# Modulation tiles on GpSimd, ScalarE and VectorE in place of TensorE in a two-layer trunk, and a first feed-forward with wide gate and up

## Chip, core and metric

The kernel runs on one core of a Trainium2 chip. Its time is the device time of one execution in microseconds (us), as the median of three runs. The engines are TensorE (PE in the profile; PEld is its weight load), VectorE (DVE), ScalarE (ACT) and GpSimd (POOL); SyncE's queue (SP) issues the DMAs of the weights. TensorE writes to banks of PSUM; everything else lies in SBUF.

## The reference

One sequence of 256 positions with 1024 channels in fp32 goes through two layers. Layer 0 is a mixer (a state-space half and an attention half with one output projection) and a gated feed-forward; layer 1 is a convolution module and another such feed-forward. Ahead of every sub-layer the norm is modulated by a vector c, and its output is gated by it:

```
mod = silu(c) @ mod_w + mod_b          # per layer: 6 sections of 1024 (shift, scale, gate, twice)
h = rms_norm(x, g) * (1 + scale) + shift
x = x + gate * sub_layer(h)

# conv feed-forward, 2816 hidden channels
a = causal_dwconv(h @ w_gate, conv_w, conv_b)     # width 3
y = (silu(a) * (h @ w_up)) @ w_down
```

So mod_w takes 1024 x 6144 weights of each layer for one row of results: a weight is read once and used once. Every 128 outputs of a section are one tile here.

## The kernel before

**Weights.** All weights come as chunks of 128x1024 fp32 (512 KB), in the sequence of `chunk_order` (line 89), into `raw` buffers (10, and later four more cut from the tiles `ABT`). `pump` (line 604) issues the next load on SyncE's queue as soon as a buffer is given back by `done`. For fp32 accuracy a chunk is split: ScalarE copies it to a rounded upper part (`whi`, or `whim` in six-slot stages), VectorE subtracts that from the chunk (`wlo`, `wlom`), and the buffer is free. TensorE then multiplies the upper part by both parts of the activations and the lower part by the upper one.

**Narrow and wide.** `tile_mm` (697) does this with three matmuls of 256 columns into 256 columns of a bank. `tile_wide` (704) does the first two as one matmul of 512 columns into a 512-wide bank; its two halves are added when the bank is emptied. Before, ffn1's gate and up are wide, ffn0's narrow.

**Gate and up.** A feed-forward has 22 pairs of a gate and an up column (the first three columns go through `lead`, the other 41 through `run_seq`). Four banks rotate. For a gate, ScalarE copies the bank to `g` and VectorE does two taps of the convolution (`ac`); for an up, VectorE multiplies the bank by `ac` (`uu`), and ScalarE and VectorE split the product into `hv`, which the down projection reads.

**Modulation.** A chunk of mod_w has one of two forms. An "mp" chunk holds rows: `mod_pe` (664) multiplies it on TensorE with silu(c) (`csv`) as the stationary operand, two matmuls of 512 columns a chunk; `mod_evac` copies the result to `mrow`, and `mod_sel` turns it into columns of `modv` by 8 small matmuls. The mixer has 24 mp chunks (three sections). An "md" chunk holds the transpose: `mod_dve` (651) multiplies it on VectorE by `cb` (silu(c) on every partition), with the sum of every row accumulated straight into a column of `modv`. ffn0 has 32 md chunks among its weights, ffn1 8.

**Order.** The class Plan records all operations of a part, gives them costs and ranks, and `arrange` (490) writes one fixed list for every engine, in which an operation's group name may add a number from the table `BONUS` to its rank. On the chip each engine executes its list in order, waiting where an operand isn't there.

Of the kernel before, what the change touches and what calls it, by code (L numbers as in the profile page):

```python
# [12 lines left out]
F32 = mybir.dt.float32  # L13
# [3 lines left out]
OP = mybir.AluOpType  # L17
# [7 lines left out]
RAW_BUFS = 10  # L25
# [10 lines left out]
MD_STEP = (2, 1)  # L36
LN_MODS = [(1, 3), (1, 4)]
# [31 lines left out]
BONUS = {'a-evac': 335.5, 'a-gate_tail': -31, 'a-h_u': 30.1, 'a-lead': 1098.9, 'a-low': -73.8, 'a-mod_dve': -8, 'a-modulate': 1999.9, 'a-norm_r': -982.9, 'a-norm_y': 306, 'a-post': 445.1, 'a-pump': 954.6, 'a-split_hi': -425.7, 'a-up_tail': 66.2, 'ab0': -12.4, 'ab1': 314.2, 'abt0': 146.2, 'abt1': -30.4, 'b': 279, 'b-low': -73, 'b-mod_dve': -176.4, 'b-post': 911.4, 'b-split_hi': -11, 'b-up_tail': 886.8, 'c-conformer': -25.6, 'c-low': -9.1, 'c-mod_dve': -195.6, 'c-norm_gain': 25.4, 'c-pump': 219.6, 'c-residual': 320.9, 'c-shift_cols': 229.2, 'c-split_hi': 308.1, 'c-stat_acc': -1.4, 'c-stat_sq': 101.1, 'c-warm': -558.3, 'ca0': -152.1, 'ca1': -12.7, 'clear0': 157.9, 'clear1': -261, 'clear2': -759.1, 'clear4': 44.9, 'cond': -26.1, 'cond0': -12.1, 'cond1': 42.8, 'cond2': 691.8, 'd-first': -7, 'd-h_u': -580.7, 'd-lead_evac': -586.6, 'd-low': 4.5, 'd-modulate': 635.9, 'd-norm_r': 37.7, 'd-norm_y': -60.3, 'd-post': -2.9, 'd-pump': -138.1, 'd-split_hi': 154.2, 'd-tap': -33.8, 'drive0': 1.6, 'drive1': -4.5, 'e-conformer': 85.9, 'e-conv_get': -2.1, 'e-conv_pe': -40.1, 'e-first': 81.1, 'e-last': -52.8, 'e-low': 930.5, 'e-post': 456.3, 'e-pump': 891.4, 'e-split_hi': -462.7, 'e-tap': -6.2, 'e-warm': 194.3, 'exp0': 1252.5, 'exp2': 21.4, 'exp3': -345.5, 'f-centre': 2, 'f-conformer': 9.6, 'f-conv_pe': 446.2, 'f-stat_sq': 551.5, 'feat0': 57.3, 'feat1': -197.8, 'feat2': -30.4, 'feat3': 36.9, 'feat4': 24.8, 'feat5': 605.8, 'feat6': 5.8, 'feat7': 416.6, 'fin0': 397.6, 'fin1': 2.4, 'fin2': 50.6, 'fin3': 2.6, 'g-conformer': -42.5, 'g-ffn_open': 117.6, 'g-h_u': -3, 'g-low': 5.9, 'g-mod_evac': -461.8, 'g-mod_sel': 153.6, 'g-norm_gain': 93, 'g-norm_y': 146.6, 'g-raw_h': -0.7, 'g-residual': 1.4, 'g-shift_cols': 5.7, 'g-silu': -1090.8, 'g-split_hi': 479.6, 'g-stat_acc': 1.7, 'g-stat_sq': 51.3, 'g-warm': -23.3, 'gelu': 585.4, 'glub0forbin': -413.2, 'gneg': 205.2, 'h-evac': -6.5, 'h-gate_tail': 1.1, 'h-h_u': -76.3, 'h-lead': -618.6, 'h-low': -370.8, 'h-modulate': 34.2, 'h-norm_r': -20.3, 'h-norm_y': -12.8, 'h-post': -171.7, 'h-pump': -339.6, 'h-split_hi': -7.9, 'h-up_tail': 9.5, 'i-gate_tail': -2.7, 'i-mod_dve': -975.6, 'i-post': -1.7, 'i-pump': -16.6, 'i-split_hi': -142.8, 'i-up_tail': -1.1, 'j-ffn': 118.4, 'j-finish': -2.7, 'j-low': -4.4, 'j-norm_y': 10.7, 'j-pump': -302, 'j-residual': -1.8, 'j-split_hi': -44.7, 'j-stat_acc': 2.3, 'j-stat_sq': 12.3, 'j-warm': -6, 'k_evac1': -9.9, 'k_evac2': -1.3, 'k_evac3': -335.2, 'kd': 9.3, 'loada000': 8500, 'loada001': 8400, 'loada010': 8200, 'loada011': 8100, 'loada020': 7900, 'loada021': 7800, 'loada030': 7600, 'loada031': 7500, 'loada040': 7200, 'loada041': 7100, 'loada050': 6900, 'loada051': 6800, 'loada060': 6600, 'loada061': 6500, 'loada070': 6300, 'loada071': 6200, 'loadabo0': -405.2, 'loadabo1': 81.4, 'loadabo2': 3.3, 'loadabo3': -114.5, 'loadabo4': 1631.5, 'loadabo6': 873.6, 'loadabo7': 639.8, 'loadanti': 29.1, 'loadbc': 7300, 'loadc': 9500, 'loadglu0': 978.9, 'loadglu1': -21.6, 'loadid': 9499, 'loadk0': 547.5, 'loadk2': 27.5, 'loadk3': -47.2, 'loadmp02': -5.7, 'loadmp04': -2.6, 'loadmp13': -566.2, 'loadmp14': 62.4, 'loadpp': 8600, 'loadsel': 9498, 'loaduq0': 8300, 'loaduq1': 8000, 'loaduq2': 7700, 'loaduq3': 7400, 'loaduq4': 7000, 'loaduq5': 6700, 'loaduq6': 6400, 'loaduq7': 6100, 'loadv0': 14.3, 'loadv1': -17.3, 'loadv3': -1548.8, 'loadx0': 9000, 'loadx1': 8900, 'loadx2': 8800, 'loadx3': 8700, 'main0': -164.3, 'main2': -8.5, 'main3': 451.8, 'main4': -14, 'main5': 1.2, 'main6': -581.6, 'main7': 334.9, 'mod_evac': 206.6, 'mod_pe004': -918.1, 'mod_pe048': -322.3, 'mod_pe1': -2043.3, 'mod_pe2': 329.2, 'mod_sel': -10.5, 'mods0': -34, 'mods1': 38.1, 'mods2': 124.4, 'mods3': -9.3, 'mods4': 662.6, 'mods5': -1.9, 'mods6': 23.2, 'mods7': 909.6, 'norm': 145.2, 'norm0': 28.9, 'norm2': 757.3, 'norm3': 4.6, 'out0': -31.3, 'out1': 223.1, 'out3': 13.8, 'poles': -82.2, 'powers': 11, 'proj_k0': 328.4, 'proj_k1': 867.2, 'proj_k2': 38.7, 'proj_k3': -5.7, 'proj_o4firstrue': -1097.9, 'proj_o5': 0.3, 'proj_v0': -1856.4, 'proj_v1': 126.3, 'proj_v2': 30.2, 'proj_v3': -27.8, 'q_evac': 594.3, 'rel': 10.1, 'res0': 6.4, 'res1': 73.3, 'res3': 272.4, 'res4': -210.4, 'rot0': -161.2, 'rot1': -1.6, 'rot2': -1.8, 'score0': -405.2, 'score1': 774.7, 'score2': -648.6, 'score3': -9, 'set': 365.8, 'skip': -738.2, 'splitabo4': 198.9, 'splitabo5': -114.3, 'splitabo6': -1.7, 'splitabo7': -2, 'splitglu1': 472.4, 'splitk1': 258.3, 'splitk3': 63.3, 'splitv0': -27.5, 'splitv1': -12.3, 'splitv3': 231.8, 'sq0': 614.4, 'sq1': 573.3, 'sq2': 839.8, 'sq3': -0.7, 'state': -231.2, 'turn0': -5.9, 'turn1': 10, 'turn3': -406.8, 'u201': -353.5, 'u_evac': -80.8, 'y0': -1280.6, 'y1': -876.8, 'y2': -545.4, 'y3': -191.1}  # L69
# [19 lines left out]
def chunk_order():  # L89
# [7 lines left out]
    def mp(l, s):  # L97
        return [("mp", l, s, f) for f in range(8)]

    a, b, c = mp(0, 2), mp(0, 4), mp(0, 3)  # L100
    order += [("k", 0), ("k", 1)] + a[:4] + [("k", 2), ("k", 3)] + a[4:]
    order += [("v", 0), ("v", 1)] + b[:4] + [("v", 2), ("v", 3)] + b[4:] + c
    order += [("abo", 4), ("abo", 5), ("glu", 0), ("glu", 1)]
# [174 lines left out]
class Plan:  # L278
# [74 lines left out]
    def cost(self, op):  # L353
        eng, fn, a, k, _ = op
        if fn == "dma_start":
            b = self.size(a[0]) * a[0].shape[0] * 4
            return max(1.0 if op[4] == "rel" else 0.06, b / 370e3)
# [191 lines left out]
class Emit:  # L549
    def __init__(self, ctx, tc, nc, d, order):  # L550
# [13 lines left out]
        self.raw = {}  # L564
        self.slots = {}
# [84 lines left out]

    def mod_dve(self, c):
# [820 lines left out]
    def ffn(self, l, mids={}):  # L1472
        nc, v = self.nc, self.nc.vector
        hv = self.hv
        def post(c, ps):
# [3 lines left out]
            if t == "gate":  # L1479
                nc.scalar.activation(g[:, 2:], ps[:, 0:T], AF.Copy)  # L1480
                if l == 1:
                    ps = g[:, 2:]
                    v.tensor_tensor(ps, psw[:, T:2 * T], ps, op=OP.add)
                self.gate_tail(l, i, ps)
            else:
                if l == 1:
                    nc.scalar.activation(u, ps[:, T:2 * T], AF.Copy)
                    v.tensor_tensor(u, ps[:, 0:T], u, op=OP.add)
                    ps = u
# [5 lines left out]
        self.run_seq(ffn_seq(l)[3:], self.h, post, mids=mids, wide=("gate", "up") if l == 1 else ())  # L1495
# [274 lines left out]
    def start(self):  # L1770
# [31 lines left out]
        nc.group = ""  # L1802

# [14 lines left out]
    def mixer0(self, ctx):  # L1818
# [3 lines left out]
        with self.tc.tile_pool(name="mix", bufs=1) as mix:  # L1822
# [11 lines left out]
            self.arena = t([128, ARENA], F32, name="arena")  # L1834
            self.cut = 0
# [30 lines left out]
            self.split(("k", 2))  # L1866
            nc.group = "proj_k1"
# [11 lines left out]
            nc.group = "mod_pe004"  # L1879
            self.mod_pe(fg, 0, fb, 0, 4)  # L1880
# [200 lines left out]
```

## Time and profile before

| what | us |
|---|---|
| median of 3 runs (their range) | 650.72 (647.98 to 651.05) |
| profiled execution, its own time | 652.1 |
| span of the profile | 650.3 |
| TensorE busy | 640.4 |
| VectorE busy | 538.8 |
| ScalarE busy | 404.9 |
| GpSimd busy | 41.2 |

The span is that of one execution between its first and its last instruction; 1.8 us lie around it. Busy times are unions over the span. The mixer ends at about 137 us, ffn0's gate and up run from about 160 to 282, its down projection to 344, the convolution module to 464, ffn1's gate and up from 473 to 583. Because a helper records every operation, almost all rows carry one line (L487); groups are told apart by the names of tiles, `out<-in`.

### The profile page before, as it was taken

How to read it: one execution, taken by the hardware profiler on the slowest of the kernel's cores; microseconds unless marked ns; L12 is line 12 of the kernel's file. 1: busy time of each engine (PE TensorE's matmuls, PEld its weight loads, DVE VectorE, ACT ScalarE, POOL GpSimd, SP SyncE). 2: the span in 40 equal slices, each digit the busy share in tenths (PEclk: the TensorE clock that was granted, in tenths of full speed). 3: DMA queues.
4: the chain of work that ended last, by engine and by line, in shares of the span. 5: the costliest groups of instructions: out<-in, count | busy, mean ns of one | idle time of the engine just before them, and what ended most of it. 6: DMA issues, size and time to landing. Idle time of an engine off the chain costs nothing.

```text
span 650.3 us, 13240 instructions
## 1 busy us (share of the span) xinstructions
PE 640.4 (98%) x5128; PEld 562.5 (87%) x5128; DVE 538.8 (83%) x1059; ACT 404.9 (62%) x736; POOL 41.2 (6%) x99
## 2 busy tenths in 40 slices
PE   8999999999999999999999999999999999999995
PEld 5789876899999999998899987568988888888885
DVE  8698996389999999999657999559999998997641
ACT  3479528897966666654446843377687766675431
POOL 4830000000000000000000222000000000000000
PEclk9999999999999999999999999999999999999998
DMA  8996888765489999999662798496476668764001
GB/s 325 405 377 224 291 324 300 316 217 210 134 288 320 325 331 303 338 328 365 195 196 81 245 325 245 154 380 263 135 280 199 201 214 259 217 210 164 1 0 66
DMA packets 45702, 158.50 MB, mean 244 GB/s; under 512 B 5535, under 2 KB 7112, under 8 KB 45640
## 3 DMA queue, kind: packets, MB, share of 16 engines
q1 hardware_dynamic: 43912, 153.84, 67.6%
q0 software_dynamic: 1152, 3.49, 1.9%
q8 instruction: 40, 0.66, 0.4%
q10 hardware_dynamic: 576, 0.33, 0.2%
q14 instruction: 22, 0.18, 0.1%
HBM read 153.10 MB, written 1.06 MB: 237 GB/s over the span
## 4 chain that ended last, share of the span: by engine, by line
PE 88%; DVE 7%; ACT 2%; DMA 1%; issue 1%; DVEq 0%; SPq 0%
PE bank L487 88%; DVE arena L487 4%; DVE wlo L487 1%; DMA raw<-w_in 1%; ACT CA L487 1%; DVE CS L487 1%; DVE U L487 1%; ACT whi L487 0%; ACT ABT L487 0%; DVE gp L487 0%; DVE nm L487 0%; DVE junk L487 0%; DVE h L487 0%; DVEq L2044 0%; DVE nt L487 0%
## 5 line engine op out<-in xcount | busy, mean ns | idle before, releaser
L487 PE MATMUL bank<-h,whi 128*128 128x256 f32 (+2 forms) x960 | 202.3, 303 | 0.2
L487 PEld LDWEIGHTS bank<-h,whi 128*128 128x128 f32 x960 | 152.4, 189 | 8.7 <-issue 1.0
L487 PE MATMUL bank<-h,wlo 128*128 128x256 f32 (+1 forms) x560 | 155.5, 283 | 0.0
L487 PE MATMUL bank<-h,whim 128*128 128x256 f32 (+1 forms) x664 | 149.1, 311 | 0.0
L487 PE MATMUL bank<-h,wlom 128*128 128x256 f32 x416 | 116.4, 281 | 0.0
L487 PEld LDWEIGHTS bank<-h,whim 128*128 128x128 f32 x664 | 108.2, 189 | 7.7
L487 PEld LDWEIGHTS bank<-h,wlo 128*128 128x128 f32 x560 | 104.5, 189 | 1.3 <-DVE CS L487 0.8
L487 DVE TENSOR_TENSOR wlo<-raw,whi 128x1024 fp32r<-128x1024 f32 x69 | 84.1, 1222 | 13.6 <-ACT whi L487 10.4
L487 ACT ACTIVATE whi<-raw 128x1024 fp32r<-128x1024 f32 x69 | 72.5, 1055 | 20.7 <-PE bank L487 13.7
L487 DVE TENSOR_TENSOR wlom<-raw,whim 128x1024 fp32r<-128x1024 f32 x60 | 72.9, 1222 | 10.5 <-ACT whim L487 10.3
L487 PEld LDWEIGHTS bank<-h,wlom 128*128 128x128 f32 x416 | 78.3, 188 | 0.1
L487 ACT ACTIVATE whim<-raw 128x1024 fp32r<-128x1024 f32 x60 | 62.6, 1054 | 22.7 <-PE bank L487 15.8
L487 PE MATMUL bank<-hv,whim 128*128 128x512 f32 (+1 forms) x236 | 67.7, 351 | 0.0
L487 PE MATMUL bank<-hv,whi 128*128 128x512 f32 x160 | 56.3, 393 | 0.0
L487 PE MATMUL bank<-hv,wlom 128*128 128x256 f32 x192 | 53.9, 281 | 0.0
L487 PEld LDWEIGHTS bank<-hv,whim 128*128 128x128 f32 x236 | 41.3, 189 | 6.2
L487 PE MATMUL bank<-hv,wlo 128*128 128x256 f32 x160 | 44.7, 279 | 0.0
L487 DVE SCALAR_TENSOR_TENSOR ac<-g,pp,ac 128x256 f32<-128x256 f32 x88 | 42.2, 482 | 2.5 <-ACT ac L487 0.8
L487 DVE SCALAR_TENSOR_TENSOR x<-bank,modv,x 128x256 f32<-128x256 f32 x54 | 25.6, 481 | 19.7 <-PE bank L487 19.1
L487 ACT ACTIVATE whi<-ABT 128x1024 fp32r<-128x1024 f32 x28 | 29.3, 1054 | 16.3 <-PE bank L487 15.3
L487 ACT ACTIVATE g<-bank 128x256 f32<-128x256 f32 x40 | 15.3, 382 | 36.4 <-PE bank L487 36.3
L487 PEld LDWEIGHTS bank<-hv,wlom 128*128 128x128 f32 x192 | 36.4, 190 | 0.0
(220 smaller groups left out, 1071.6 us busy)
## 6 DMA issues: line engine op xcount, KB each, us to landing
raw<-w_in SPq DMA_DIRECT2D x213, 512.0 KB, 5.3
ABT<-w_in SPq DMA_DIRECT2D x71, 512.0 KB, 4.9
a<-ap POOLq DMA_DIRECT2D x24, 142.0 KB, 5.4
x<-x_in SPq DMA_DIRECT2D x4, 256.0 KB, 4.2
arena<-scr SPq DMA_DIRECT2D x1, 1024.0 KB, 6.0
cb<-c_in SPq DMA_DIRECT2D x2, 512.0 KB, 4.9
kT<-bc_in SPq DMA_DIRECT2D x1, 512.0 KB, 11.4
out<-junk SPq DMA_DIRECT2D x2, 256.0 KB, 2.0
```

The lines of the kernel that those rows point to most:

```text
L487: getattr(getattr(self.nc, eng), fn)(*a, **k)
```

## The change

In the mixer the 24 mp chunks become md chunks, spread among the weights of k, v, the output projection and the gate of the state-space half. `mod_next` places them one by one among the mixer's groups. Of every three, two go through the new `mod_pool`: GpSimd multiplies the chunk by `cbm` in place, then ScalarE copies it onto itself with the sum of every row accumulated into `modv`. The third is a VectorE multiplication with accumulation, as in `mod_dve`. That is 16 tiles on GpSimd and ScalarE, 8 on VectorE; `mod_pe`, `mod_evac` and `mod_sel` go from the mixer. `broadcast` makes `cbm` at the start, with one VectorE instruction, two matmuls and two ScalarE copies, and the room for it is taken from the raw buffers (9 for 10).

In both feed-forwards every second md chunk goes through `mod_pool`: 16 of 32 in ffn0, 4 of 8 in ffn1. ffn0's gate and up use `tile_wide`, with the addition of the halves as in ffn1: one more VectorE instruction for a gate, and one more of VectorE and of ScalarE for an up. The planner's cost of a DMA changes from 370 to 390 KB a us, and most numbers of the table `BONUS` are new.

```diff
-RAW_BUFS = 10
+RAW_BUFS = 9
...
+MIX_MOD = (1, 1, 0)
+ON_POOL = (1, 0)
...
-    a, b, c = mp(0, 2), mp(0, 4), mp(0, 3)
-    order += [("k", 0), ("k", 1)] + a[:4] + [("k", 2), ("k", 3)] + a[4:]
-    order += [("v", 0), ("v", 1)] + b[:4] + [("v", 2), ("v", 3)] + b[4:] + c
-    order += [("abo", 4), ("abo", 5), ("glu", 0), ("glu", 1)]
+    md = [("md", 0, s, f) for s in (2, 4, 3) for f in range(8)]
+    for c, n in zip([("k", 0), ("k", 1), ("k", 2), ("k", 3), ("v", 0), ("v", 1), ("v", 2), ("v", 3),
+                     ("abo", 4), ("abo", 5), ("glu", 0), ("glu", 1)], (1, 1, 1, 1, 2, 2, 2, 2, 3, 3, 3, 3)):
+        order += [c] + md[:n]
+        del md[:n]
...
-            return max(1.0 if op[4] == "rel" else 0.06, b / 370e3)
+            return max(1.0 if op[4] == "rel" else 0.06, b / 390e3)
...
-                (self.mod_dve if c[0] == "md" else self.split)(c)
+                (self.mod if c[0] == "md" else self.split)(c)
...
+    def mod(self, c):
+
+        self.i_mod += 1
+        (self.mod_pool if ON_POOL[self.i_mod % len(ON_POOL)] else self.mod_dve)(c)
+        if c[3] == 7:
+            self.mod_bias(*c[1:3])
+
+    def mod_pool(self, c):
+        _, l, s, f = c
+        w = self.raw[c]
+        self.nc.gpsimd.tensor_tensor(w, w, self.cb, op=OP.mult)
+        self.nc.scalar.activation(w, w, AF.Copy, accum_out=self.modv[l][:, s * 8 + f:s * 8 + f + 1])
+        self.done(c)
+
+    def mod_next(self, n):
+        for _ in range(n):
+            i = self.i_next
+            self.nc.group = "mod%d" % i
+            c = ("md", 0, (2, 4, 3)[i // 8], i % 8)
+            if MIX_MOD[i % len(MIX_MOD)]:
+                self.mod_pool(c)
+            else:
+                w = self.raw[c]
+                self.nc.vector.scalar_tensor_tensor(w, w, 1.0, self.cb, op0=OP.mult, op1=OP.mult,
+                                                    accum_out=self.modv[0][:, c[2] * 8 + c[3]:c[2] * 8 + c[3] + 1])
+                self.done(c)
+            self.i_next += 1
...
-                if l == 1:
-                    ps = g[:, 2:]
-                    v.tensor_tensor(ps, psw[:, T:2 * T], ps, op=OP.add)
+                ps = g[:, 2:]
+                v.tensor_tensor(ps, psw[:, T:2 * T], ps, op=OP.add)
...
-        self.run_seq(ffn_seq(l)[3:], self.h, post, mids=mids, wide=("gate", "up") if l == 1 else ())
+        self.run_seq(ffn_seq(l)[3:], self.h, post, mids=mids, wide=("gate", "up"))
...
+    def broadcast(self):
+
+        nc = self.nc
+        cb = self.cb.rearrange("p (a b) -> p a b", b=128)
+        nc.vector.tensor_tensor(cb, self.ident.unsqueeze(1).to_broadcast([128, 8, 128]),
+                                self.cs.unsqueeze(2).to_broadcast([128, 8, 128]), op=OP.mult)
+        parts = (0, 4, self.aux[2]), (4, 8, self.aux[1])
+        for a, b, ps in parts:
+            nc.tensor.matmul(ps, self.ones, self.cb[:, a * 128:b * 128], start=True, stop=True)
+        for a, b, ps in parts:
+            nc.scalar.activation(self.cb[:, a * 128:b * 128], ps, AF.Copy, scale=float(D))
...
             self.split(("k", 2))
+            self.mod_next(2)
             nc.group = "proj_k1"
...
-            nc.group = "mod_pe004"
-            self.mod_pe(fg, 0, fb, 0, 4)
+            self.mod_next(1)
             nc.group = "proj_k2"
...
             nc.group = "score0"
             self.attn_score(0, B[0:2])
+            self.mod_next(2)
             nc.group = "proj_v3"
```

GpSimd's list in the mixer, from the end of the constants of the state-space half (`D`) to the turn of the bias table (the COPY of `arena`), before and then after the change:

```order
L487 COPY D_127<-arena 128x1024
L487 MEMSET D_127 128x16
L487 COPY arena<-arena 128x8x128
L487 MEMSET g_0_1641 128x2
```

```order
L491 COPY D_126<-arena 128x1024
L491 MEMSET D_126 128x16
L491 TENSOR_TENSOR raw_75<-raw_75,cbm 128x1024
L491 TENSOR_TENSOR raw_77<-raw_77,cbm 128x1024
L491 TENSOR_TENSOR raw_72<-raw_72,cbm 128x1024
L491 TENSOR_TENSOR raw_74<-raw_74,cbm 128x1024
...
L491 TENSOR_TENSOR ABT_87<-ABT_87,cbm 128x1024
L491 COPY arena<-arena 128x8x128
L491 TENSOR_TENSOR ABT_86<-ABT_86,cbm 128x1024
```

Ten multiplications now stand ahead of the COPY, the first two ahead of the copies of u on ScalarE, and six behind it.

ScalarE's list at the same place: `kT` and `KD` are the attention's keys and a table of the state-space half, `whi_78<-raw_69` the split of v's first chunk, the rows with `modv` the accumulations of `mod_pool`. Before and after:

```order
L487 ACTIVATE kT<-bank_65 128x256 x2
L487 ACTIVATE U_122<-u 32x4x64 x9
L487 ACTIVATE KD<-bank_65 32x16x32 x4
L487 ACTIVATE whi_79<-raw_69 128x1024
L487 ACTIVATE whi_83<-raw_71 128x1024
```

```order
L491 ACTIVATE raw_72,modv_89<-raw_72 128x1024
L491 ACTIVATE kT<-bank_65 128x256 x2
L491 ACTIVATE raw_77,modv_89<-raw_77 128x1024
L491 ACTIVATE raw_76,modv_89<-raw_76 128x1024
L491 ACTIVATE KD<-bank_65 32x16x32 x4
L491 ACTIVATE raw_74,modv_89<-raw_74 128x1024
L491 ACTIVATE raw_75,modv_89<-raw_75 128x1024
L491 ACTIVATE ABT_87,modv_89<-ABT_87 128x1024
L491 ACTIVATE whi_78<-raw_69 128x1024
```

Accumulations stand between and ahead of what was consecutive before: ten ahead of the split of v's first chunk, four of them earlier than these rows.

VectorE's list in ffn0's gate and up, about one pair (`ac`: the taps of the gate, `wlom`: splits, `junk,modv`: a modulation tile, `hv`: the product's lower part), before and after:

```order
L487 SCALAR_TENSOR_TENSOR ac_1643<-g_0_1641,pp,ac_1643 128x256 x2
L487 TENSOR_TENSOR wlom_1634<-ABT_87,whim_1633 128x1024
L487 TENSOR_TENSOR uu_1645<-bank_62,ac_1643 128x256
L487 SCALAR_TENSOR_TENSOR junk,modv_90<-raw_75,cb 128x1024
L487 TENSOR_TENSOR hv<-uu_1645,hv 128x256
L487 TENSOR_TENSOR wlom_1636<-raw_78,whim_1635 128x1024
L487 SCALAR_TENSOR_TENSOR junk,modv_90<-raw_69,cb 128x1024
```

```order
L491 TENSOR_TENSOR g_0_1627<-bank_61,g_0_1627 128x256
L491 TENSOR_TENSOR wlom_1620<-raw_71,whim_1619 128x1024
L491 SCALAR_TENSOR_TENSOR ac_1629<-g_0_1627,pp,ac_1629 128x256 x2
L491 TENSOR_TENSOR uu_1631<-bank_62,uu_1631 128x256
L491 SCALAR_TENSOR_TENSOR junk,modv_90<-raw_74,cb 128x1024
L491 TENSOR_TENSOR uu_1631<-uu_1631,ac_1629 128x256
L491 TENSOR_TENSOR wlom_1622<-raw_73,whim_1621 128x1024
L491 TENSOR_TENSOR hv<-uu_1631,hv 128x256
```

Two sums of bank halves (`g<-bank,g` and `uu<-bank,uu`) come into a pair, and about every second modulation tile goes out of it. In all 11 such tiles stand in gate and up after the change; 12 of ffn0's 16 GpSimd multiplications stand ahead of the last `hv`.

## Rows read from the trace of the kernel before

**Rows 1.** The page, parts 1 and 4: busy time by engine, the chain by engine.

```profile
PE 640.4 (98%) x5128; PEld 562.5 (87%) x5128; DVE 538.8 (83%) x1059; ACT 404.9 (62%) x736; POOL 41.2 (6%) x99
...
PE 88%; DVE 7%; ACT 2%; DMA 1%; issue 1%; DVEq 0%; SPq 0%
```

**Rows 2.** The chain in order of time: start, length (us), what.

```profile
44.81 1.06 ACT CA L487
...
90.05 1.15 DVE wlo L487
91.24 328.39 PE bank L487 x2956
```

**Rows 3.** Stretches of the span: length, busy us of each engine, clock, DMA.

```profile
core 0: us, PE busy (x) PEld busy (x) DVE busy (x) ACT busy (x) POOL busy (x), PEclk, DMA share, GB/s
45.00:57.00 12.00, 12.00 (x100) 10.99 (x97) 9.55 (x21) 11.86 (x20) 0.00 (x0) 1.00 0.87 319
...
57.00:100.10 43.10, 43.01 (x358) 33.63 (x360) 41.97 (x83) 22.44 (x48) 1.10 (x1) 1.00 0.73 257
100.00:137.00 37.00, 37.00 (x510) 30.15 (x501) 17.70 (x43) 30.75 (x78) 0.00 (x0) 0.95 0.80 301
160.00:282.00 122.00, 122.00 (x1024) 121.82 (x1023) 120.83 (x204) 82.51 (x144) 0.00 (x0) 1.00 0.85 291
282.00:344.00 62.00, 62.00 (x382) 55.47 (x382) 46.51 (x69) 30.06 (x41) 0.08 (x1) 1.00 0.77 263
473.00:583.00 110.00, 110.00 (x629) 96.12 (x628) 102.77 (x181) 80.11 (x148) 0.00 (x0) 1.00 0.70 225
```

**Rows 4.** Timeline of GpSimd (POOL) and VectorE (DVE): start, length (us).

```profile
28.21 0.22 POOL L487 TENSOR_TENSOR arena<-arena 128x16 f32<-128x16 f32 x1
...
28.56 0.96 POOL L487 TENSOR_SCALAR arena<-arena 128x16 f32<-128x16 f32 x1
...
28.41 1.00 DVE L487 TENSOR_TENSOR arena<-arena 128x768 f32<-128x768 f32 x1
...
37.48 1.11 POOL L487 COPY D<-arena 128x1024 f32<-128x1024 f32 x1
...
37.80 0.81 DVE L487 SCALAR_TENSOR_TENSOR gp<-modv,gneg 128x1 f32<-128x1 f32 x1
...
27.83 0.15 DVE L487 SCALAR_TENSOR_TENSOR gp<-modv,gneg 128x1 f32<-128x1 f32 x1
```

**Rows 5.** ScalarE's groups, 100 to 137 us: count, busy us, mean ns.

```profile
L487 ACT ACTIVATE whi<-raw 128x1024 fp32r<-128x1024 f32 x4 | 4.2, 1056 | 2.5 <-PE bank L487 1.3 <-DMA raw<-w_in 1.2
...
L487 ACT ACTIVATION_READ_ACCUMULATOR CS<-CS,U 128x1 f32 x11 | 2.1, 190 | 0.0
```

**Rows 6.** Instructions with csv (PE, PEld, ACT, POOL), then mrow (PE, PEld, DVE, ACT).

```profile
100.00:137.00 37.00, 4.49 (x42) 0.97 (x32) 0.00 (x0) 0.00 (x0) 0.95 0.80 301
...
100.00:137.00 37.00, 2.07 (x16) 2.02 (x16) 0.00 (x0) 1.05 (x2) 0.95 0.80 301
```

**Rows 7.** Instructions with cb (DVE, ACT), then with a bank (PE, PEld, DVE, ACT).

```profile
160.00:282.00 122.00, 30.66 (x50) 1.04 (x1) 1.00 0.85 291
...
473.00:583.00 110.00, 8.69 (x15) 0.35 (x1) 1.00 0.70 225
...
57.00:100.10 43.10, 43.01 (x358) 33.63 (x360) 7.00 (x12) 7.90 (x19) 1.00 0.73 257
...
473.00:583.00 110.00, 110.00 (x629) 96.12 (x628) 17.05 (x41) 15.25 (x41) 1.00 0.70 225
```

**Rows 8.** Timeline of ScalarE: gates in ffn0 (eleven), then in ffn1 (nine).

```profile
204.49 0.39 ACT L487 ACTIVATE g<-bank 128x256 f32<-128x256 f32 x1 [1.42 <-PE bank L487]
...
261.44 0.39 ACT L487 ACTIVATE g<-bank 128x256 f32<-128x256 f32 x1 [1.40 <-PE bank L487]
...
503.49 0.39 ACT L487 ACTIVATE g<-bank 128x256 f32<-128x256 f32 x1 [0.89 <-PE bank L487]
...
548.42 0.39 ACT L487 ACTIVATE g<-bank 128x256 f32<-128x256 f32 x1
```

More of the change, by code (lines that the diff above doesn't have):

```diff
@@ L98, in mp @@
         return [("mp", l, s, f) for f in range(8)]
-    a, b, c = mp(0, 2), mp(0, 4), mp(0, 3)
-    order += [("k", 0), ("k", 1)] + a[:4] + [("k", 2), ("k", 3)] + a[4:]
-    order += [("v", 0), ("v", 1)] + b[:4] + [("v", 2), ("v", 3)] + b[4:] + c
-    order += [("abo", 4), ("abo", 5), ("glu", 0), ("glu", 1)]
+    md = [("md", 0, s, f) for s in (2, 4, 3) for f in range(8)]
[3 more added lines that the diff above has]
+        del md[:n]
+    assert not md
     order += [("abo", i) for i in (6, 7, 0, 1, 2, 3)]
@@ L564, in __init__ @@
         self.raw = {}
+        self.i_mod = 0
+        self.i_next = 0
         self.slots = {}
@@ L646, in feed, with mod_bias @@
                     break
-                (self.mod_dve if c[0] == "md" else self.split)(c)
+                (self.mod if c[0] == "md" else self.split)(c)
             self.pos += 1
         self.auto = True
+    def mod(self, c):
[22 more added lines that the diff above has]
+            self.i_next += 1
+    def mod_bias(self, l, s):
+        mc = self.modcols(l, s)
+        self.nc.vector.tensor_tensor(mc, mc, self.par("modb", l * 48 + s * 8, 8), op=OP.add)
     def mod_dve(self, c):
@@ L656, in mod_dve @@
         self.done(c)
-        if f == 7:
-            mc = self.modcols(l, s)
-            self.nc.vector.tensor_tensor(mc, mc, self.par("modb", l * 48 + s * 8, 8), op=OP.add)
     def low(self, n):
@@ L1480, in post @@
                 nc.scalar.activation(g[:, 2:], ps[:, 0:T], AF.Copy)
-                if l == 1:
-                    ps = g[:, 2:]
-                    v.tensor_tensor(ps, psw[:, T:2 * T], ps, op=OP.add)
+                ps = g[:, 2:]
+                v.tensor_tensor(ps, psw[:, T:2 * T], ps, op=OP.add)
                 self.gate_tail(l, i, ps)
             else:
[L1486 to L1489, printed above, removed]
+                nc.scalar.activation(u, ps[:, T:2 * T], AF.Copy)
+                v.tensor_tensor(u, ps[:, 0:T], u, op=OP.add)
+                ps = u
                 nc.scalar.activation(a, a, AF.Silu)
@@ L1784, in start @@
             nc.tensor.matmul(self.mm[i % 4][:, 0:n], self.zero[:, 0:128], self.zero[:, 0:n], start=(i < 4), stop=False)
+        nc.group = "bcast"
+        self.broadcast()
         nc.group = "poles"
@@ L1834, in mixer0 @@
             self.arena = t([128, ARENA], F32, name="arena")
+            self.cb = t([128, 1024], F32, name="cbm")
             self.cut = 0
@@ L1889, in mixer0 @@
             self.pump()
+            self.mod_next(1)
             nc.group = "proj_k3"
             self.proj_k(3)
-            nc.group = "mod_pe048"
-            self.mod_pe(fg, 0, fb, 4, 8)
+            self.mod_next(1)
             nc.group = "splitv0"
@@ L1899, in mixer0 @@
             self.k_evac(3)
+            self.mod_next(1)
             nc.group = "splitv1"
@@ L1912, in mixer0 @@
             vb = B[4:6]
+            self.mod_next(1)
             nc.group = "proj_v0"
@@ L1916, in mixer0 @@
             self.split(("v", 2))
+            self.mod_next(1)
             nc.group = "proj_v1"
@@ L1920, in mixer0 @@
             self.split(("v", 3))
-            nc.group = "mod_pe1"
-            self.mod_pe(fg, 1, fb)
+            self.mod_next(2)
             nc.group = "proj_v2"
             self.proj_v(2, vb)
+            self.mod_next(1)
             nc.group = "score0"
             self.attn_score(0, B[0:2])
+            self.mod_next(2)
             nc.group = "proj_v3"
@@ L1931, in mixer0 @@
                 nc.scalar.activation(self.v[:, t_, :], vb[t_], AF.Copy)
-            nc.group = "mod_pe2"
-            self.mod_pe(fg, 2, fb)
+            self.mod_next(1)
             nc.group = "exp0"
             self.attn_exp(0, B[0:2])
+            self.mod_next(1)
             nc.group = "norm0"
@@ L1939, in mixer0 @@
             self.attn_score(1, B[2:4])
-            nc.group = "mod_evac"
-            self.mod_evac(fb)
+            self.mod_next(1)
             nc.group = "exp1"
             self.attn_exp(1, B[2:4])
+            self.mod_next(1)
             nc.group = "y0"
             self.s5_y(0, B[4])
-            nc.group = "mod_sel"
-            self.mod_sel(fg, B[0])
+            self.mod_next(1)
             nc.group = "norm1"
@@ L1951, in mixer0 @@
             self.attn_turn(0, (B[6], B[7]))
+            self.mod_next(1)
             nc.group = "y1"
             self.s5_y(1, B[5])
+            self.mod_next(1)
             nc.group = "out0"
             self.attn_out(0, B[1])
+            self.mod_next(1)
             nc.group = "score2"
             self.attn_score(2, B[2:4])
+            self.mod_next(1)
             nc.group = "exp2"
             self.attn_exp(2, B[2:4])
+            self.mod_next(1)
             nc.group = "turn1"
             self.attn_turn(1, (B[6], B[7]))
+            self.mod_next(1)
             nc.group = "y2"
@@ L1965, in mixer0 @@
             self.attn_norm(2)
+            nc.group = "mod_bias"
+            for i in (2, 4, 3):
+                self.mod_bias(0, i)
             nc.group = "out1"
```

2 lines of the change are left out of this document (1 added, 1 removed).

## The prediction

> **What bounds the kernel now.** I read the page first, then the chain of waits in order of time, then the busy time of each engine by stretches, because averages over the span mix stages with different limits. By the page TensorE is busy for 98% of the span and the chain runs over it for 88% [rows 1], which invites the thought that work taken off TensorE shortens the kernel by its own length. The chain in order of time says something else for the first 91 us: up to there its pieces are ScalarE's (the row at 44.81 us is the first of a run of them) and then VectorE's, and only from 91.24 us on is TensorE alone on it for 328 us [rows 2]. The stretches agree. Between 57 and 100 us VectorE is busy for 41.97 of 43.10 us; from 100 to 137 us it is at 17.70 of 37.00, with ScalarE at 30.75; in the first feed-forward's gate and up (160 to 282 us) TensorE is at 122.00 of 122.00 and VectorE at 120.83, so there two engines are full at once; in the down projection (282 to 344) and in ffn1 (473 to 583) VectorE has room, 15.5 and 7.2 us [rows 3]. So VectorE has 1.1 us to spare in each of the two stretches where the change puts work beside it.
>
> **What a GpSimd instruction costs VectorE.** The trace of before has almost no GpSimd work, but what it has meets VectorE. A TENSOR_TENSOR of 16 elements takes 0.22 us; a TENSOR_SCALAR of the same size that begins 0.15 us after a VectorE instruction with two operands in SBUF takes 0.96, and ends (28.56 + 0.96 = 29.52) 0.11 us after that one (28.41 + 1.00). The other way round, while GpSimd's COPY of 128x1024 runs (37.48 + 1.11 = 38.59), a VectorE instruction on one column takes 0.81 us in place of its 0.15, and ends at 38.61 [rows 4]. I read this as one access that both need and that one instruction holds to its end. Then a multiplication on GpSimd is not free for VectorE: it costs VectorE the time T that it holds the access, less what VectorE can do meanwhile with operands from a bank.
>
> T has no row, so it is bounded. The COPY streams 1024 elements in 1.11 − 0.22 = 0.9 us [rows 4]. If the multiplication streams as the COPY does, T = 0.9; if its two reads and its write follow one another, 2.7; with the two reads in turn and the fixed part, 2 × 0.9 + 0.2 = 2.0. I take 2.0, since the COPY has one read and the multiplication two.
>
> The Trainium skill bears on this in two places, and both speak against the change. "SBUF — State Buffer", section "Who interferes with whom", says that the pair of ports that VectorE and GpSimd share is locked for a whole instruction, and that a VectorE instruction with two SBUF inputs meets a GpSimd one that reads SBUF; the trace agrees for the small instructions above, and no row shows it for a multiplication. "GPSIMD Engine Reference", section "3.1 Elementwise — side-by-side cycle accounting", gives 4497 ns for a tensor_tensor of 2048 elements on GpSimd; half of it, an estimate of 2.25 us, would put the sum below 4 us higher.
>
> By T = 2.0 a tile that goes to GpSimd holds VectorE for some 1.6 us, while the same tile on VectorE takes 1.23 (30.66 us for 25 pairs of multiplication and accumulator read [rows 7]).
>
> **The mixer.** TensorE loses 4.49 us of modulation matmuls after 100 us and 2.07 of the selection [rows 6], 6.6 in all; those ahead of 91 us lie beside VectorE's chain and give nothing. VectorE gains 8 tiles, GpSimd 16, and ScalarE 16 accumulations of 1.06 + 0.19 = 1.25 us (a 128x1024 ACTIVATE and an accumulator read [rows 5]). Where they fall I take from the order of the instructions.
> - 45 to 57 us: two GpSimd multiplications, whose accumulations stand on ScalarE ahead of the copies of u. ScalarE is at 11.86 of 12.00 [rows 3] and on the chain [rows 2], so these two cost 2 × 1.25 = **+2.5**. VectorE has 2.5 us idle there, which hides the 3.2 us of their hold but for less than a microsecond, beside ScalarE's delay.
> - 57 to 100 us: eight more stand ahead of GpSimd's COPY of the bias table, and VectorE takes one tile. A hold doesn't stop VectorE's instructions with a bank operand, 7.00 of its 41.97 us [rows 7], nor its few reductions, so I charge 0.8 of T: 8 × 2.0 × 0.8 = 12.8, plus 1.2, less the 1.1 idle: **+12.9**. ScalarE is at 22.44 of 43.10 and takes its eight accumulations in that room.
> - 100 to 137 us: TensorE gives 6.6 back if nothing else is late. VectorE has room for its seven tiles (17.70 + 8.6). ScalarE gets four accumulations and loses 1.05 of evacuation: 30.75 + 5.0 − 1.05 = 34.7 of 37, so no more than **−2.3** can be had.
>
> Together +13.1. The broadcast at the start is a VectorE multiplication of 128x1024, two matmuls and two ScalarE copies; at most 1.2 [rows 7] + 2 × 0.5 [rows 6] = 2.2 us with its matmuls beside that, if all of it were on the chain; a gain is excluded, since it only adds work. The chain there is TensorE's, so I take 0. One raw buffer less costs 0 as long as the queue stays ahead; its cover is the buffers loaded ahead, and without it the chunks come late (the fourth case below).
>
> **ffn0.** A pair of gate and up takes (261.44 − 204.49)/10 = 5.695 us narrow, and in the wide form of ffn1 (548.42 − 503.49)/8 = 5.616 [rows 8]. For 20.5 pairs TensorE needs 115.1 in place of 116.7 us, **−1.6**. VectorE in the wide form: ffn1's 102.77 less 8.69 of modulation [rows 3, 7] is 94.1 over 110/5.616 = 19.6 pairs, 4.80 a pair, so 98.4 for 20.5; this holds the added sums of the halves, since ffn1 has them. By the order 11 tiles stay on VectorE inside gate and up, 11 × 1.23 = 13.5, and 12 stand on GpSimd ahead of the last product: 12 × 2.0 × 0.83 = 19.9 (0.83 is what is left beside the bank operands, 17.05 of 102.77 [rows 3, 7]). Sum 131.8, over TensorE's 115.1 by 16.7. Four banks rotate, so TensorE can be three ahead, 1.5 pairs or 8.4 us, and that much of the lag is taken up in the down projection, where VectorE has 15.5 us of room. 16.7 − 8.4 = 8.3 remain; with −1.6 the stage is **+6.7**. The down projection itself (4 tiles on each engine, +3 us on VectorE against 15.5 of room) and ffn1 (4 of 8 tiles moved, +1.7 against 7.2) cost 0.
>
> **Sum.** The profiled execution took 652.1 us; 652.1 + 13.1 + 6.7 = 671.9. The median of the runs is 1.4 lower, so 670.5, rounded to **670**.
>
> **The rivals.**
> 1. *No hold.* The multiplication doesn't block VectorE, or VectorE slips its work between. Then VectorE's 98.4 + 13.5 = 111.9 stays below TensorE's 115.1 and the mixer keeps TensorE's saving: −2.3 − 1.6, that is 648.2, or 647 by the median; with all 6.6 back, 642.5. For it speaks that most GpSimd instructions of before are too small to tell. Against it speaks the column instruction above, which waited out the whole COPY. It decides below T of about 0.6 us, where 8 × 0.8 × T makes up the 3.9 gained. This is the one on the other side.
> 2. *Hold as short as the COPY's*, T = 0.9: mixer 5.8 + 0.1 + 2.5 − 2.3 = +6.1; in ffn0 111.9 + 9.0 = 120.9 is 5.8 over TensorE, which the banks absorb, −1.6. 656.6, or 655 by the median. For it: the only 1024-element rows of GpSimd; against: those have one input.
> 3. *Everything in turn*, T = 2.7, nothing absorbed by the banks and nothing saved by TensorE, because ScalarE executes in order: its accumulations wait for GpSimd, with the copies for v's splits behind them, and a raw buffer comes back only after both engines, so the queue of weights runs late. Mixer 17.3 + 0.1 + 2.5 = +19.9; ffn0 138.8 − 115.1 − 1.6 = +22.1: 694.1, or 693 by the median. For it: ten accumulations stand on ScalarE ahead of the copy for v's first split. Against: ScalarE is at half in that stretch [rows 3].
>
> **How the numbers follow.** I give the forecast 0.54, the first rival 0.23, the second 0.13, the third 0.10. A difference of 0.5% (3.3 us) is about what a measurement of this kernel can tell from none. The forecast and the third are slower; of the second 0.08 is slower and 0.05 the same; of the first 0.20 is faster and 0.03 the same. So slower 0.72, same 0.08, faster 0.20. The range goes from 643, which takes in most of the first rival, to 690, which leaves out the upper end of the third.
>
> **What would show it.** Right: GpSimd multiplications of about 2 us, VectorE's two-operand instructions behind them that end with them and are stretched by as much, VectorE's pieces on the chain past 91 us and again in the gate and up, and a pair period there of 6 us or more. The mixer's last VectorE piece would come some 13 us later. Wrong: VectorE's 1024-element subtractions still at 1.22 us beside running multiplications (no hold), or a pair period of 5.6 us; ScalarE with long waits for GpSimd and the loads late would be the third rival. My forecast fails most easily on T and on the share of the holds that falls where VectorE has no room.

## The result and the profile after

The changed kernel takes 699.12 us (median of four runs, 695.61 to 703.06) against 650.84 for the kernel before: a ratio of 1.0754, with a 95% interval from 1.0683 to 1.0826. It is slower by 48 us, where 20 were forecast, and lies outside the range of 643 to 690.

The page of the profiled execution (its span is 699.3 us) shows TensorE no longer full and its share of the chain down from 88% [rows 1] to 55%. By itself that share doesn't show a loss: in the first experiment below it is 63%, at 651 us. VectorE gains 68 us of busy time.

```profile
PE 645.8 (92%) x4692; PEld 555.2 (79%) x4692; DVE 607.0 (87%) x1077; ACT 445.1 (64%) x829; POOL 152.1 (22%) x135
...
PE 55%; DVE 19%; ACT 5%; issue 3%; DMA 1%; DVEq 0%; SPq 0%; ACTq 0%
```

The stretches that answer to [rows 3], and ffn0's gate and up where they now lie (206 to 332), columns as there:

```profile
45.00:57.00 12.00, 6.29 (x46) 5.06 (x44) 11.41 (x22) 11.06 (x18) 10.16 (x9) 0.85 0.46 176
57.00:100.10 43.10, 36.15 (x307) 33.94 (x307) 41.78 (x55) 26.57 (x52) 17.63 (x7) 0.88 0.71 246
100.00:137.00 37.00, 22.44 (x193) 17.69 (x196) 36.90 (x54) 19.07 (x50) 15.92 (x6) 0.72 0.47 167
206.00:332.00 126.00, 117.99 (x636) 100.49 (x634) 123.72 (x182) 85.27 (x160) 32.22 (x11) 0.96 0.74 256
```

VectorE is as full from 57 to 100 us as it was, but gets through 55 instructions in place of 83. The full stretch doesn't end there: from 100 to 137 us, where it was half idle, it is now busy for 36.90 of 37.00, and TensorE waits. In gate and up it is full too, and TensorE is not.

The timelines of GpSimd and VectorE at the first three multiplications show why (start, length in us; the row with x3 is three in a row):

```profile
48.28 7.01 POOL L491 TENSOR_TENSOR raw<-raw,cbm 128x1024 f32<-128x1024 f32 x3
...
48.54 2.17 DVE L491 TENSOR_TENSOR arena<-CS,arena 128x16 f32<-128x16 f32 x1
50.74 2.28 DVE L491 TENSOR_TENSOR CS<-arena 128x16 f32<-128x16 f32 x1
53.06 2.36 DVE L491 TENSOR_TENSOR arena<-CS,arena 128x16 f32<-128x16 f32 x2
55.45 0.19 DVE L491 TENSOR_TENSOR CS<-arena 128x16 f32<-128x16 f32 x1
```

VectorE has products of 16 elements to do, 0.19 us each when nothing is in the way (55.45). Each of them waits out a whole multiplication, gets through in the gap, and the next meets the next multiplication. The wait is counted as length of the waiting instruction, so VectorE looks busy: an average of the group hides it, the shape gives it away. The split of 128x1024 that stood behind them came at 56.76 us in place of 50.59 in the first experiment below. A split that meets a multiplication is stretched in the same way, here to 3.44 us; most don't meet one (the 14 of wlom<-raw in gate and up have a mean of 1214 ns), so a split at 1.22 us is no sign of a missing hold:

```profile
215.14 2.42 POOL L491 TENSOR_TENSOR ABT<-ABT,cb 128x1024 f32<-128x1024 f32 x1 [21.95 <-DMA ABT<-w_in]
...
215.20 3.44 DVE L491 TENSOR_TENSOR wlo<-raw,whi 128x1024 fp32r<-128x1024 f32 x1
```

In gate and up the same is seen in VectorE's groups (206 to 332 us; count, busy us, mean ns):

```profile
L491 DVE TENSOR_TENSOR hv<-uu,hv 128x256 fp32r<-128x256 f32 x21 | 17.3, 826 | 0.9 <-ACT hv L491 0.6
...
L491 DVE TENSOR_TENSOR uu<-uu,ac 128x256 f32<-128x256 f32 x19 | 14.5, 764 | 0.1
...
L491 DVE TENSOR_TENSOR g<-bank,g 128x256 f32<-128x256 f32 x20 | 8.3, 416 | 0.7 <-ACT g L491 0.6
L491 DVE TENSOR_TENSOR uu<-bank,uu 128x256 f32<-128x256 f32 x20 | 8.3, 414 | 0.0
```

The two forms that read both operands from SBUF went to 764 and 826 ns (422 and 421 in the first experiment); the two of the same size with one operand in a bank stayed at 416 and 414. On GpSimd the shortest of the 36 multiplications takes 2.35 us (least, median and greatest time in ns of thirteen of the mixer's sixteen):

```profile
L491 POOL TENSOR_TENSOR raw<-raw,cbm x13: 2352/2529/3330, 48.3 to 153.2; 128x1024 f32<-128x1024 f32 x13
```

GpSimd is held up as well: thirteen in the feed-forwards (raw<-raw,cb) have a mean of 2931 ns.

### The profile page after: what moved, and what is told of

Read it like the earlier page. It is cut to its first block, busy times and chain, and to the rows that moved or that the text cites. A ratio compares the mean times of both kernels' runs of the same rounds, so it can differ in the third digit from the quotient of the medians.

```text
span 699.3 us, 12509 instructions
## 1 busy us (share of the span) xinstructions
PE 645.8 (92%) x4692; PEld 555.2 (79%) x4692; DVE 607.0 (87%) x1077; ACT 445.1 (64%) x829; POOL 152.1 (22%) x135
## 4 chain that ended last, share of the span: by engine, by line
PE 55%; DVE 19%; ACT 5%; issue 3%; DMA 1%; DVEq 0%; SPq 0%; ACTq 0%
PE bank L491 55%; DVE wlo L491 4%; DVE uu L491 3%; DVE ac L491 3%; DVE wlom L491 2%; DVE hv L491 2%; DVE junk L491 2%; DVE h L491 1%; DMA raw<-w_in 1%; ACT whi L491 1%; DVE g L491 1%; ACT whim L491 1%; ACT h L491 1%; ACT L491 1%; ACT raw L491 0%
## 5 line engine op out<-in xcount | busy, mean ns | idle before, releaser
L491 PEld LDWEIGHTS bank<-h,whi 128*128 128x128 f32 x800 | 136.4, 195 | 28.8 <-DVE h L491 8.0
L491 PE MATMUL bank<-h,whim 128*128 128x512 f32 (+1 forms) x496 | 151.1, 365 | 5.7 <-DVE h L491 2.6
L491 PEld LDWEIGHTS bank<-h,whim 128*128 128x128 f32 x496 | 89.4, 191 | 22.4 <-DVE h L491 3.1
L491 DVE TENSOR_TENSOR wlo<-raw,whi 128x1024 fp32r<-128x1024 f32 x74 | 94.2, 1279 | 8.5 <-ACT whi L491 8.2
L491 ACT ACTIVATE whi<-raw 128x1024 fp32r<-128x1024 f32 x74 | 77.6, 1054 | 28.0 <-PE bank L491 24.5
L491 POOL TENSOR_TENSOR raw<-raw,cb 128x1024 f32<-128x1024 f32 x13 | 38.1, 2931 | 128.9 <-DMA raw<-w_in 103.5
L491 ACT ACTIVATE whim<-raw 128x1024 fp32r<-128x1024 f32 x53 | 55.5, 1052 | 8.3 <-PE bank L491 7.1
L491 DVE SCALAR_TENSOR_TENSOR ac<-g,pp,ac 128x256 f32<-128x256 f32 x88 | 46.1, 526 | 1.0 <-ACT ac L491 0.2
L491 POOL TENSOR_TENSOR raw<-raw,cbm 128x1024 f32<-128x1024 f32 x13 | 33.6, 2604 | 52.1 <-DMA raw<-w_in 52.1
L491 DVE SCALAR_TENSOR_TENSOR x<-bank,modv,x 128x256 f32<-128x256 f32 x54 | 25.3, 480 | 20.3 <-PE bank L491 19.6
L491 POOL TENSOR_TENSOR ABT<-ABT,cb 128x1024 f32<-128x1024 f32 x7 | 20.9, 2991 | 92.3 <-DMA ABT<-w_in 69.8
## 6 DMA issues: line engine op xcount, KB each, us to landing
arena<-scr SPq DMA_DIRECT2D x1, 1024.0 KB, 11.6
```

The lines of the kernel that those rows point to most:

```text
L491: getattr(getattr(self.nc, eng), fn)(*a, **k)
```

## The experiments

The theory is the hold: a GpSimd multiplication keeps VectorE's instructions with two SBUF operands out for as long as it reads. The first rival is ScalarE's queue: its accumulations wait for GpSimd, and the splits behind them with them. Others are the new order of the start, the broadcast, the wide form, and the length of VectorE's own work. All runs but two keep every instruction in the list of the changed kernel at its place and exchange or leave out instructions only when the finished list is written out, so that order can't explain a difference. Each time is one run; the kernel before took 649.3 to 650.8 beside them. Where a product is replaced it is left out of the result too.

**GpSimd writes only, or does nothing.** Where the list is written out:

```diff
+if eng == "gpsimd" and fn == "tensor_tensor" and self.size(a[0]) == 1024:
+    for n in (1024, 1024, 512):
+        self.nc.gpsimd.memset(a[0][:, 0:n], 0.0)
+    continue
```

> The changed kernel with every instruction of every engine in its place, but each of the 36 multiplications of 128x1024 on GpSimd is replaced by three MEMSETs of the same chunk (1024, 1024 and 512 elements), which take GpSimd about as long (estimate 2.3 to 2.5 us) and read nothing. The product is left out, so these modulation columns are zero. If the hold costs the time (GpSimd's reads shut VectorE's two-operand instructions out), VectorE's instructions fall back to their plain durations and the kernel to 655 to 670 us, the pair period in ffn0 to 5.6 to 5.8. If ScalarE's queue behind GpSimd costs it, GpSimd takes as long as before and the time stays at 694 to 703, the pair period above 6.2.

Measured: **651.07**, the whole 48 us gone and 4 below the range of the first case. GpSimd's three MEMSETs take 0.95, 0.95 and 0.53 us, 2.4 a tile, as long as the multiplication at its least (2.35, though its median is 2.53 in the row above, since it is held up too), and ScalarE still waits for them. VectorE's groups in gate and up (206 to 285 us of this run) are back at their lengths:

```profile
L495 DVE TENSOR_TENSOR wlo<-raw,whi 128x1024 fp32r<-128x1024 f32 x10 | 12.2, 1219 | 0.7 <-ACT whi L495 0.7
...
L495 DVE TENSOR_TENSOR hv<-uu,hv 128x256 fp32r<-128x256 f32 x14 | 5.9, 421 | 1.1 <-ACT hv L495 0.9
```

So it is not GpSimd's time that costs, but its reading; and the start's order, the broadcast, nine raw buffers, the wide form and ScalarE's wait come, together with what TensorE is spared, to nothing that can be measured. No run parts these from one another.

> The same order again, but GpSimd's 36 multiplications are left out altogether, so ScalarE accumulates the bare chunk as soon as it has landed; the product is left out of the result. Both theories say faster than the changed kernel. If the hold alone costs the time, this equals the run with MEMSETs within 4 us. If ScalarE's wait for GpSimd costs it, this run alone falls to 655 to 670 and the one with MEMSETs doesn't. What both keep over the kernel before is neither: the order of the start, the broadcast, the wide form.

The edit is the first without its MEMSETs. Measured: **644.47**, 6.6 below the run with MEMSETs, where the theory allowed 4. The mixer's first residual comes at 144.9 us against 149.9. Waiting for GpSimd is therefore real and costs some 5 us in the mixer, a tenth of the whole; the rest is the hold and what follows from it. Whether the 5 us come by ScalarE's queue or by weights that come later because a buffer is given back later isn't parted here: the chain of the run with MEMSETs has accumulations behind MEMSETs on it, and two waits of 5.9 and 6.8 us for weights. This is also the most that the idea could have given in this order: with multiplications free of charge, 6 us under the kernel before.

**By stage.** The same MEMSETs for the feed-forwards' tiles alone, then for the mixer's alone (`and not group.startswith("mod")` in the condition of the first edit, and without the `not`).

> The changed kernel in its order, with GpSimd's real multiplications in the mixer alone (16); the 20 of the feed-forwards are replaced by the MEMSETs of the first run, so their modulation columns are zero. By the landmarks of the changed kernel against the run with all MEMSETs, the first residual of the mixer comes 25.7 us later. If each stage pays its own holds: 651 + 26 = 675 to 680. If the mixer's lateness is given back (later stages catch up on weights loaded meanwhile): 660 to 670.

> The reverse: MEMSETs in the mixer, real multiplications in the two feed-forwards (20). If the stages are independent, 48 - 26 = 22 over the run with all MEMSETs: 670 to 676, and ffn0's gate and up keep their 126 us from the first gate to the last up. If that stage is slow only because it follows a slow mixer, 655 to 662. My forecast for this part alone, with three banks taking up 8.4 us, would give 658 to 660.

Measured: **676.61** and **672.28**, 25.5 and 21.2 over the run with all MEMSETs. They add up to 46.7 of the 48, well within the changed kernel's own range of 7 us: each stage pays its own, and nothing is given back later. In the second run the time from ffn0's first gate to its last up is 125.9 us (178.2 to 304.1) against 109.3 with MEMSETs, though the mixer ahead of it was quick.

**By length.** Half of the columns multiplied, with two MEMSETs of 512 behind; then a COPY of the chunk onto itself behind MEMSETs of 1024 and 512.

```diff
...
+    self.nc.gpsimd.tensor_tensor(a[0][:, 0:512], a[1][:, 0:512], a[2][:, 0:512], op=OP.mult)
+    for n in range(2):
+        self.nc.gpsimd.memset(a[0][:, 512:1024], 0.0)
...
```

> All 36 multiplications over 512 of the 1024 columns, and two MEMSETs of 512 columns behind each, so that GpSimd takes about as long; the product of the other half is left out. If the holds count from the first microsecond, half of the 48: 671 to 679. If banks and slack take up the first part, as the forecast had it for ffn0 (8.4 us there), less than half: 655 to 667.

> All 36 multiplications replaced by two MEMSETs (1024 and 512 elements) and a COPY of the chunk onto itself, in the same order; GpSimd takes about as long (estimate 2.5 us), of which only the COPY of 1.04 us reads. The product is left out. If every reading instruction holds VectorE for its length, 1.04 of 2.35 us: 651 + 0.44 x 48 = 668 to 676, like the run with half of the columns. If only two reads at once hold it, 649 to 655. If each event costs a fixed delay whatever its length, 690 to 700.

Measured: **672.60** and **662.71**, the second under its 668. The first lies in the upper case by its number, but not all of its 21.5 us over the run with MEMSETs is the hold's: its start is slow, with a granted clock of 0.58 from 10 to 20 us and 0.74 from 20 to 30, where the run with MEMSETs has 1.00 in both (columns as in [rows 3]):

```profile
10.00:20.00 10.00, 9.63 (x72) 7.03 (x72) 6.08 (x43) 1.73 (x4) 0.00 (x0) 0.58 1.03 411
20.00:30.00 10.00, 9.92 (x80) 7.78 (x81) 6.28 (x33) 4.38 (x12) 7.15 (x25) 0.74 0.90 325
```

TensorE is as busy there as in the other run (19.6 and 19.4 us of 20), and why its clock is lower is not shown. VectorE's first nt<-x,gp,bank comes at 24.9 us in place of 19.0, so 5.9 us are lost before the first of the 36 tiles; less these it is 666.7 (an estimate), in the lower case. Behind the mixer's first residual, too, half the columns cost 7.5 us and the whole multiplications 24.3, less than half. So "half of the 48" isn't borne out. One read is enough to hold VectorE (17.7 us more of busy time with the COPY), but the COPY cost less than its length told. The lengths and VectorE's busy time on the four pages show how a hold is counted:

| GpSimd reads for | least time of one (us) | VectorE busy (us) | added for each of 36 (us) | kernel over 651.07 (us) | of that behind the mixer's first residual (us) |
|---|---|---|---|---|---|
| nothing (MEMSETs) | 0 | 541.1 | 0 | 0 | 0 |
| COPY | 1.04 | 558.8 | 0.49 | 11.6 | 7.7 |
| half multiplication | 1.28 | 569.3 | 0.78 | 21.5 (slow start) | 7.5 |
| multiplication | 2.35 | 607.0 | 1.83 | 48.0 | 24.3 |

A hold costs VectorE here its length less about 0.5 us (0.55, 0.50, 0.52). The 20 tiles behind the first residual give the same without the start: 0.50, 0.79 and 1.89 a tile. Of the time so added 0.66 (COPY) and 0.73 (multiplication) ends up in the kernel's. (The last column and VectorE's times are those of the profiled executions; the changed kernel's took 701.16 us, 50.1 over the run with MEMSETs.) The forecast of the COPY's run took the cost as proportional to the length; that half a microsecond is what it missed.

**The same tiles on VectorE.** Each of the 36 as one VectorE multiplication with accumulation, standing where ScalarE's accumulation stood; then that for the feed-forwards' 20 alone, with the mixer's 16 left on GpSimd.

```diff
+if eng == "gpsimd" and fn == "tensor_tensor" and self.size(a[0]) == 1024:
+    self.cbs = getattr(self, "cbs", {})
+    self.cbs[id(a[0])] = a
+    continue
+if fn == "activation" and id(a[0]) in getattr(self, "cbs", {}) and "accum_out" in k:
+    w, _, cb = self.cbs.pop(id(a[0]))
+    self.nc.vector.scalar_tensor_tensor(w, w, 1.0, cb, op0=OP.mult, op1=OP.mult, accum_out=k["accum_out"])
+    continue
```

> All other instructions in the order of the changed kernel, but each of the 36 tiles is one VectorE multiplication with accumulation, standing where ScalarE's accumulation stood; GpSimd and ScalarE do nothing for them. If a hold of about 2.4 us at a share of 0.8 costs VectorE more than the 1.23 us of its own instruction, some 0.7 us a tile is saved and the time is 672 to 686. If the place in VectorE's list matters more than the length (as the run with the feed-forwards' tiles on VectorE, which was no faster than the changed kernel, suggests), 692 to 703.

> The changed kernel in its order, the 16 multiplications of the mixer on GpSimd; the 20 tiles of the feed-forwards that were GpSimd's are VectorE's, each where ScalarE's accumulation stood. The run that planned the same distribution anew took 699, with up to three modulation tiles in a row ahead of a bank's emptying. If VectorE's load in the wide form is what costs there, 692 to 700 again. If the order is what costs, this is the mixer's 676 plus what these stages cost in the run with all tiles in place, from the first residual to the end 508.5 against 499.4 with MEMSETs, so 9 more: 682 to 688.

Measured: **669.93**, 2 under its first case and 29 us faster than with GpSimd's help: to have GpSimd do a tile costs VectorE more than to do it (by busy time, 1.83 us a tile against 0.99: 576.8 us in this run, 541.1 with MEMSETs). And **690.76**, between its two cases, 3 above the second and 1 below the first. The second is the one that its parts bear out: from the first residual on it needs 507.9 us, as the 508.5 expected; its first residual (181.1 us) is 5.4 to 7.5 us later than in the four other kernels with this mixer, and this began at the start: its granted clock is 0.58 from 10 to 20 us and 0.74 from 20 to 30, as in the run with half multiplications, where the run with the mixer's holds alone shows 1.00 in both. Its first nt<-x,gp,bank comes at 25.1 us, 6.2 late; less these it is 684.6 (an estimate), in the second case.

**Two newly planned kernels.** With the feed-forwards' tiles on VectorE (`ON_POOL = (0,)`), the first also with ffn0 narrow as before, the second with the wide form:

> The change in the mixer alone: ffn0 narrow and all modulation tiles of both feed-forwards on VectorE, as before. By the landmarks of the two traces the changed kernel is 33 us late at ffn0's first gate, of which some 5 come between the mixer's end and there, and 16.5 more at the last up. If both stages count in full, 679 to 684; if the mixer's delay is partly given back by a later stage that no longer lags, 670 to 678.

> The changed kernel, mixer and wide form included, with all modulation tiles of the feed-forwards on VectorE. If a tile on GpSimd holds VectorE for longer than the 1.23 us that VectorE needs for it, this is faster than the changed kernel, by about 12 x (2.4 x 0.83 - 1.23) = 9 us in gate and up: 688 to 694, a pair period of about 6.1. If GpSimd does relieve VectorE and the wide form is what costs, it is slower than the changed kernel: 703 to 712. If ScalarE's queue is what costs, it falls by the whole stage, to 680 to 684.

Measured: **675.47**, by its number the lower case, but not for its reason: the first residual comes at 173.6 us, 26.2 later than before, and 25.1 of it are left at the end, so almost nothing was given back. The 5 us that I had put between the mixer's end and ffn0 are hardly there in this kernel (25.1 us from first residual to first gate, 24.5 before and 29.5 in the changed kernel); 3 of them are the lead's two GpSimd tiles by the run with holds in the feed-forwards alone (next section), which this kernel hasn't. And **698.99**, which none of the three readings had. Since the same distribution takes 690.76 in the changed kernel's order, at least 8 of these microseconds come from the order that the planner found for it, and 15 if both are counted from the first residual on (522.7 against 507.9), which leaves the other's slow start out. VectorE's timeline there shows three modulation tiles in a row ahead of a bank that waits to be emptied:

```profile
243.53 1.22 DVE L491 SCALAR_TENSOR_TENSOR junk<-raw,cb 128x1024 f32<-128x1024 f32 x1
...
244.79 1.22 DVE L491 SCALAR_TENSOR_TENSOR junk<-ABT,cb 128x1024 f32<-128x1024 f32 x1
...
246.06 1.22 DVE L491 SCALAR_TENSOR_TENSOR junk<-raw,cb 128x1024 f32<-128x1024 f32 x1
...
247.21 0.42 DVE L491 TENSOR_TENSOR uu<-bank,uu 128x256 f32<-128x256 f32 x1
```

No run beats the kernel before with all its work done, and the run without multiplications puts the prize at 6 us.

## Why the prediction was right in kind and wrong in size

The mechanism held: a reading GpSimd instruction holds the access, VectorE is what pays, and the kernel is slower. The sum was 28 us short. Point by point:

- *T = 2.0.* The least is 2.35 us, above my sum of two streams. (The Trainium skill, "GPSIMD Engine Reference", section "3.1 Elementwise — side-by-side cycle accounting", from whose figure I had estimated 2.25, was nearer, and a little low.) The share of 0.8 came out right (1.83 of 2.35 is 0.78), but by luck: I took it as the part of VectorE's work without a bank operand, so that the cost would go with the length, and the shorter reads have shares of 0.47 and 0.61. What comes off a hold here is some 0.5 us, whatever its length. Over the eight of the mixer that I charged to VectorE and ffn0's twelve, with the measured 1.83 in place of 1.60 and 1.66, this is 3.9 us.
- *The mixer, +13.1.* Its first residual came at 175.6 us in place of 147.4, 28.2 later, of which the holds make 25.7 (149.9 with MEMSETs). The step that failed is "eight more stand ahead of GpSimd's COPY": I closed VectorE's full stretch at 100 us, where it had ended before, and charged only the multiplications inside. But the stretch grows with what it takes in. GpSimd's timeline has fifteen multiplications start before 126 us, and VectorE is full to there, so five that were thought to lie in its idle time had none to lie in. Up to the first residual VectorE is busy for 158.7 us against 130.5 with MEMSETs: the sixteen tiles cost it 28.2, and 25.7 arrive there (with whatever TensorE's lower clock adds, see the last section).
- *The first two tiles, +2.5, charged to ScalarE.* Three came in a row, on the small instructions of VectorE shown above. ScalarE's first copy of u is at 63.7 us against 57.5 with MEMSETs: 6.2, and VectorE's.
- *TensorE's −2.3.* With MEMSETs the mixer's first residual comes 2.5 us later than before, without them 2.5 earlier. A saving of that size shows, in sum with the new order and the broadcast, but the wait for GpSimd, which I put into the third rival alone, takes 5.0, twice as much.
- *ffn0's lead*, charged at nothing: two multiplications lie in it (187 to 193 us), and the run with holds in the feed-forwards alone has 23.0 us from the mixer's last residuals to the first gate (155.2 to 178.2) against 20.0 with MEMSETs.
- *Gate and up, +6.7.* From first gate to last up it is 126.5 us (205.2 to 331.7) against 110.0 (171.9 to 281.9): +16.5, of which the holds make 16.6 (125.9 against 109.3, above). The pair period, 6.4 us over nineteen pairs, is past the 6 that the forecast gave as a sign. VectorE's time was forecast at 131.8 for 20.5 pairs, and it is 123.72 for twenty. The step that failed is the 8.4 us that "is taken up in the down projection": from the last up to the down projection's first residual it is 9.0 us now and was 7.1, so nothing was taken up; the stage came out near VectorE's own time. A first column of the down projection needs all hidden tiles, the last included, so banks that run ahead delay the lag but don't take it off the end. That reading of the order is argued, not tried by itself.
- *The chain's first 91 us*, read as ScalarE's and VectorE's: up to 32.5 us they are nearly all TensorE's, as the remark on the broadcast says. Nothing in the sum hangs on it.

Of the rivals, *no hold* is excluded by the first experiment and *a hold as short as the COPY's* by the lengths. *Everything in turn* came nearest in time, 693, but only part of its mechanism holds: nothing was absorbed in ffn0 and the wait for GpSimd ate TensorE's saving, while its T of 2.7 was too long, and its late weights were never tried by themselves. The Trainium skill's rule of the shared ports ("SBUF — State Buffer", section "Who interferes with whom") agrees with the runs on which instructions meet: a GpSimd instruction that only writes left VectorE's two-operand splits at 1219 ns, one that reads brought the same group (wlo<-raw) to a mean of 1362 ns.

## What to carry to other kernels

Before work goes to GpSimd, add its hold to VectorE's time and not only to GpSimd's: here a tile of 1.22 us on VectorE cost VectorE 1.83 us when GpSimd did it. By these runs an offload of this kind could pay only where VectorE is idle or reads from banks, which no run here tried. And where a stage is charged with more work, its end moves, so count what lies behind the old end too.

## What the runs showed beside that

- A stretched instruction keeps its name and shape, so a group's mean shows the hold only against the same group elsewhere (hv<-uu,hv at 826 ns and 421).
- Where TensorE waits, its granted clock is lower: it is 0.72 from 100 to 137 us, with TensorE busy for 22.44 of 37.00, against 0.95 and 37.00 before. TensorE has no work there for 12.35 us, until a split of VectorE is done at 115.0; from 105 to 115 us the clock is 0.50, its lower level, and from 120 to 125 us 1.00. A matmul of 512 columns takes twice as long at first as 8 us later:

```profile
115.01 0.80 PE L491 MATMUL bank<-wlo,h 128*128 128x512 f32 x1 [12.35 <-DVE wlo L491]
...
122.96 0.39 PE L491 MATMUL bank<-wlo,h 128*128 128x512 f32 x1
```

What this adds by itself can't be read apart from the waits that go with it.
